# A two-layer hybrid decoder trunk on one core: the first weights split in turn with x, a bank of its own for the last block's sum, and transposes inside the next product group

## The chip, the cores and the metric

The kernel runs as one program on one core of a Trainium2 chip. Its time is the device time of one execution, in microseconds (us). The core has five engines that run their own instruction lists and wait for each other through semaphores: TensorE (PE in the profile, with the weight loads apart as PEld), VectorE (DVE), ScalarE (ACT), GpSimd (POOL) and SyncE (SP). A queue that starts DMA transfers has the engine's name with a q behind it (SPq, ACTq).

## The reference

x has 256 rows of 2048 columns, all in fp32. Two layers follow each other, and each does:

```
h  = rmsnorm(x);  z = h @ w_in          # GLU pair | q, k, v | forget logits | gates A, B
yA = conv(GLU) -> layernorm -> silu -> @ w_conv_out
yB = softmax(q k^T / sqrt(d) + C[t] - C[s], causal) v -> @ w_attn_out
x += (sigmoid(gA) * yA + sigmoid(gB) * yB) @ w_out
x += swiglu(rmsnorm(x))                 # w_gate_up, w_down, 5632 hidden columns
x += sigmoid(rmsnorm(x) @ w_ple_gate) * (p[i] @ w_ple_proj)
```

A last rmsnorm ends it. The weights are some 570 MB, which is what the profile shows as read from HBM.

## The kernel before, in words

**Split products.** A product of fp32 precision is made of three matmuls of a rounded type: x is held as xh + xl, a weight piece as wh + wl, and `Sum.add` issues xh·wh, xh·wl and xl·wh (lines 184, 185, 186), each 128x128 by 128x512. A weight piece (128 x 1024 elements, 512 KB) is brought by `fetch` into one of 8 `raw` buffers and split: ScalarE writes wh (line 143), VectorE writes wl = raw - wh (line 144). There are 5 buffers for wh and 5 for wl. A piece that is used whole feeds 12 matmuls.

**PSUM.** Two tiles of two banks ("mm") hold sums of both 128-row blocks of x. Four single banks ("ms") hold everything small: transposes, attention scores, and the product sums below. All eight banks are so in use.

**Product phases.** `fast_chunks` computes two neighbouring column chunks together by a scheme of Strassen's kind: for each group it adds and subtracts quarter pieces of the weights (lines 269 and 270 on `raw` tiles, and one DMA that adds) and issues seven products of six matmuls each: p1, c21, c11, q7, q6, q5, c12. p1, q7, q6 and q5 have a single bank each, which takes all four; c11, c12 and c21, c22 share the two mm tiles. Ordinary pieces (`go`, 12 matmuls each) are put between the products. After the products, p1 is copied from its bank by ScalarE (line 289) and VectorE combines it with the q sums. Some phases have one group, some two (`FAST = (2, 1)`).

**Transposes.** A result that is to be the next stage's left operand is transposed by TensorE: 8 transposes of 128x128 (line 330) into two single banks (`turned`), which ScalarE copies as hi (line 317, or 320 with a gain, or 349 and 352 into the operands of a product group, `Fast.take`) and VectorE subtracts as lo (lines 318, 321). Such a step is put into the list `turns`, and `run()` takes one step from it. In the kernel before, `go` calls `run()` only once the products of the phase are issued (`state["quiet"]`).

**Order.** A scheduling layer reorders the instructions of each engine when the program is built, and gives out the buffers in that order; what it made is fixed in the program. Instructions of one engine run in that order.

**Opening and end.** `fetch_first` brings the first two weight pieces, the first in two halves through the ACT queue; `take` makes xh, xl from the transposed x that `load_x` brings, scaled by the norm vector `vecs`; `warm` issues matmuls on ones. The last `fast_chunks` of the program (with `by_block`) ends one 128-row block before the other, so that the last normalisation of block 0 (lines 975 to 979) runs beside block 1's matmuls. c21 and c22 are there the two banks of one tile.

Of the kernel before, what the change touches and what calls it, by code (L numbers as in the profile page):

```python
# [28 lines left out]
KD = D // P  # L29
# [3 lines left out]
FFN_PARTS = (3, 4, 4)  # L33

PAIRS = 28
WARM = 10
RAWS = 8

FAST = (2, 1)
# [8 lines left out]
def trunk(ctx, tc, xT, xR, pT, wI, wF, wC, wA, wOut, wGU, wD, wPG, wPP, vec, bF, gF, out):  # L48
# [98 lines left out]

    recent = [None]

    def fetch_first(src, hook):  # L150

        parts = []
        for half in range(2):
            raw = raws.tile([P, 2, 512], F32, tag="raw", name=f"raw{next(uid)}")
            h = whs.tile([P, 2, 512], F32R, tag="wh", name=f"wh{next(uid)}")
            l = wls.tile([P, 2, 512], F32R, tag="wl", name=f"wl{next(uid)}")
            c = half * 1024
            if half == 0:
                for k in range(2):
                    nc.scalar.dma_start(raw[:, k, :], src[:, k * 512 : (k + 1) * 512])  # L160
                warm()
                hook()
            else:
                nc.sync.dma_start(raw.rearrange("p k n -> p (k n)"), src[:, c : c + 1024])
            for k in range(2):
                act.activation(h[:, k, :], raw[:, k, :], AF.Copy)  # L166
                dve.tensor_tensor(l[:, k, :], raw[:, k, :], h[:, k, :].bitcast(F32), op=ALU.subtract)
            parts.append((h, l))
        return parts

# [28 lines left out]
    def sums_of_blocks(n1, n2=None):  # L199
        t = once(bank_mm)  # L200
        return t, Sum(n1, lambda: t()[:, 0, :]), Sum(n1 if n2 is None else n2, lambda: t()[:, 1, :])
# [11 lines left out]
            run()  # L213


    def chunk(groups, xs, hook=None):
        n = sum(len(ks) for _, ks in groups)
        if n == 2:
            sums = [Sum(n, once(bank_ms)) for _ in range(2)]
        else:  # L220
            t, *sums = sums_of_blocks(n)
        for src, ks in groups:
            if hook is not None:
                parts = fetch_first(src, hook)
                hook = None
            else:
                parts = [split(fetch(src[:, o * 512 : (o + 2) * 512])) for o in range(0, len(ks), 2)]
            await_x(xs, ks)
            for j, p in enumerate(parts):
                plain(sums, xs, ks[2 * j], p)  # L230
            run()
            fill(CONV)
        return t() if n > 2 else [b.t for b in sums]
# [4 lines left out]
    def fast_chunks(fast, w1, w2, xs, ks, first, by_block=None):  # L238
# [4 lines left out]
        p1, q5, q6, q7 = (Sum(nf, once(bank_ms)) for _ in range(4))  # L243
        c1, c11, c12 = sums_of_blocks(nf + nk)
        c2, c21, c22 = sums_of_blocks(nf + nk, nk)
        left = deque()
        for w, sums in ((w1, (c11, c12)), (w2, (c21, c22))):
            for g, k0 in enumerate(ks):
# [23 lines left out]
        for g, f in enumerate(fast):  # L272
            a11, sm = fetch(w1[g][:, :1024]), fetch(w2[g][:, :1024])
            nc.gpsimd.dma_start(sm.rearrange("p k n -> p (k n)"), w1[g][:, :1024], accum_op=ALU.add)
            a22, a12 = fetch(w2[g][:, 1024:]), fetch(w1[g][:, 1024:])
            product(p1, f(B11), a11)
            product(c21, f(N4X), a22)
            go()
            product(c11, f(B21), a12)
            if len(left) > 2 * len(ks):  # L280
                go()
            product(q7, f(T3), sm)
            add(sm, sm, a22)
            product(q6, f(T2), sm)
            sub(a11, sm, a11)
            product(q5, f(M1), a11)
            add(a12, a12, sm)
            product(c12, f(B22), a12)
# [22 lines left out]
        return [(w[g], range(4 * g, 4 * g + 4)) for g in range(n)]  # L311


    def halves(o, src, scale=None):
        hi, lo = o[..., :S], o[..., S:]
        if scale is None:
            act.activation(hi, src, AF.Copy)
            dve.tensor_tensor(lo, src, hi.bitcast(F32), op=ALU.subtract)
        else:
            act.activation(hi, src, AF.Copy, scale=scale)  # L320
            dve.scalar_tensor_tensor(lo, src, scale, hi.bitcast(F32), op0=ALU.mult, op1=ALU.subtract)

    def turned(src):

# [155 lines left out]
            xT[:, 4 * q + lo : 4 * q + hi, :].rearrange("p k s -> p (k s)"),  # L480
        )

    def take(q, lo=0, hi=4):
        for k in range(lo, hi):
            if k % 2 == 0:
                o = pair(F32R)
                norm.tiles[4 * q + k], norm.tiles[4 * q + k + 1] = o[:, 0, :], o[:, 1, :]
            norm.xs[4 * q + k] = by_blocks(norm.tiles[4 * q + k])
            halves(
                norm.tiles[4 * q + k], xin[q].rearrange("p a b -> p (a b)")[:, k * S : (k + 1) * S],  # L490
                norm.gain(4 * q + k),
            )

    load_x(0, 0, 2)
    nc.sync.dma_start(vecs[:, :KD], vec[:, :KD])

    def warm():

# [1 line left out]
        t = bank_ms()  # L500
        for _ in range(WARM):
            pe.matmul(t[:, :P], lhsT=ones, rhs=ones, start=True, stop=True)

    def hook():
        load_x(0, 2, 4)
        take(0)

    def early():
        norm.fast = [Fast()]
# [27 lines left out]
    for i in range(L):  # L537
# [4 lines left out]
        col = lambda n: vecs[:, n : n + 1]  # L542


        def project(c, hook=None):
            return chunk(by_four(wI[i, c]), norm.xs, hook)


        u, cv = [], []
# [33 lines left out]
        for hh in range(2):  # L583
            first = i == 0 and hh == 0
            if first:
                turns.append(lambda: (load_x(1), turns.append(rest(1))))
            pa = project(GLU[hh], hook if first else None)
            at, gt = pair(), pair()
            act.activation(at, pa, AF.Copy)
            pg = project(GLU[hh] + 1)  # L590
# [463 lines left out]
```

## Time and profile before

| | |
|---|---|
| time, median of 3 runs | 2826.44 us (2826.43 to 2826.75) |
| profiled execution | 2827.59 us, of it 2825.9 us span |
| mean granted TensorE clock | 0.997 |
| TensorE busy | 2803.7 us, 99% of the span |
| VectorE busy | 2345.7 us, 83% |
| ScalarE busy | 1581.5 us, 56% |

The span is what the profile covers; 1.69 us of the profiled execution lie outside it. Busy shares tell which engine is nearly always at work; where the others are waited for is told by the waits and the timeline.

### The profile page before, as it was taken

What the parts mean: (1) busy time and instruction counts of PE and PEld (TensorE: products, weight loads), DVE (VectorE), ACT (ScalarE), POOL (GpSimd) and SP (SyncE); (2) the same over time, 40 slices, a digit from 0 to 9 for tenths busy, and PEclk for the clock granted to TensorE, in tenths of its full rate; (3) what the DMA queues carried; (4) which work ended last, traced back from release to release, by engine and by line L of the source; (5) the groups of instructions that cost most, each with busy time, mean ns of one, the idle gap of its engine ahead of it and who ended that gap; (6) DMA issues with size and microseconds to landing.
All of it is one profiled execution on the core that took longest, in us unless ns stands there. A gap on an engine that the chain in (4) does not pass through costs nothing.

```text
span 2825.9 us, 34767 instructions
## 1 busy us (share of the span) xinstructions
PE 2803.7 (99%) x12684; PEld 2318.0 (82%) x12684; DVE 2345.7 (83%) x2835; ACT 1581.5 (56%) x1912; POOL 60.0 (2%) x99
## 2 busy tenths in 40 slices
PE   9999999999999999999999999999999999999998
PEld 7888788888888888888888887888888888888886
DVE  6998877777989878888869988678689889788887
ACT  6445755565556545556644457455555465455665
POOL 0000000000000000000000000000000000000000
PEclk9999999999999999999999999999999999999999
DMA  8555466566676666666655545665656676576673
GB/s 296 183 183 187 152 215 199 192 208 192 216 224 221 203 216 217 215 216 201 214 173 189 185 165 179 209 200 180 227 188 210 220 228 221 192 231 210 204 238 123
DMA packets 158428, 573.71 MB, mean 203 GB/s; under 512 B 17840, under 2 KB 18096, under 8 KB 158000
## 3 DMA queue, kind: packets, MB, share of 16 engines
q1 hardware_dynamic: 149040, 539.50, 55.7%
q0 software_dynamic: 8352, 30.41, 5.9%
q8 instruction: 99, 1.62, 0.2%
q10 hardware_dynamic: 864, 1.57, 0.2%
q14 instruction: 73, 0.60, 0.1%
HBM read 569.32 MB, written 2.10 MB: 202 GB/s over the span
## 4 chain that ended last, share of the span: by engine, by line
PE 91%; DVE 6%; ACT 1%; issue 1%; DMA 0%; SPq 0%; POOLq 0%; POOL 0%; DVEq 0%; ACTq 0%
PE mm L184 26%; PE mm L186 26%; PE mm L185 26%; PE ms L184 4%; PE ms L185 4%; PE ms L186 4%; DVE pair L561 3%; DVE wl L144 2%; PE ms L330 2%; ACT wh L143 1%; PE ms L718 0%; DVE raw L269 0%; PE ms L747 0%; PE ms L737 0%; DMA pair<-in_xT_dram 0%
## 5 line engine op out<-in xcount | busy, mean ns | idle before, releaser
L143 ACT ACTIVATE wh<-raw 128x1024 fp32r<-128x1024 f32 x1188 | 1239.9, 1059 | 1122.4 <-PE mm L186 750.7
L144 DVE TENSOR_TENSOR wl<-raw,wh 128x1024 fp32r<-128x1024 f32 x1188 | 1434.9, 1224 | 380.8 <-ACT wh L143 375.4
L184 PE MATMUL mm<-wh,pair 128*128 128x512 f32 x3452 | 1352.9, 392 | 6.1 <-ACT wh L166 3.0
L186 PE MATMUL mm<-wh,pair 128*128 128x512 f32 x3452 | 1346.0, 390 | 0.0
L185 PE MATMUL mm<-wl,pair 128*128 128x512 f32 x3452 | 1345.7, 390 | 0.3 <-DVE wl L144 0.3
L184 PEld LDWEIGHTS mm<-wh,pair 128*128 128x128 f32 x3452 | 648.8, 188 | 139.7 <-ACT wh L166 3.2
L186 PEld LDWEIGHTS mm<-wh,pair 128*128 128x128 f32 x3452 | 648.7, 188 | 135.3
L185 PEld LDWEIGHTS mm<-wl,pair 128*128 128x128 f32 x3452 | 648.9, 188 | 133.3 <-DVE wl L144 0.7
L561 DVE SCALAR_TENSOR_TENSOR pair<-pair,vecs,pair 128x256 f32<-128x256 f32 x480 | 203.6, 492 | 0.0
L184 PE MATMUL ms<-wh,pair 128*128 128x512 f32 x496 | 193.5, 391 | 1.9 <-ACT wh L143 1.9
L186 PE MATMUL ms<-wh,pair 128*128 128x512 f32 x496 | 193.1, 389 | 0.0
L185 PE MATMUL ms<-wl,pair 128*128 128x512 f32 x496 | 193.1, 389 | 0.0
L269 DVE TENSOR_TENSOR raw<-raw,raw 128x1024 f32<-128x1024 f32 x116 | 141.8, 1222 | 1.9
L184 PEld LDWEIGHTS ms<-wh,pair 128*128 128x128 f32 x496 | 93.1, 188 | 23.6 <-ACT wh L143 3.0
L186 PEld LDWEIGHTS ms<-wh,pair 128*128 128x128 f32 x496 | 93.0, 188 | 19.4
L185 PEld LDWEIGHTS ms<-wl,pair 128*128 128x128 f32 x496 | 93.1, 188 | 18.8
L269 DVE TENSOR_TENSOR pair<-pair,ms 128x512 f32<-128x512 f32 x144 | 94.2, 683 | 0.0
L270 DVE TENSOR_TENSOR pair<-mm,pair 128x1024 f32<-128x1024 f32 (+1 forms) x49 | 59.0, 1203 | 18.9 <-PE mm L186 18.9
L270 DVE TENSOR_TENSOR raw<-raw,raw 128x1024 f32<-128x1024 f32 x58 | 71.0, 1225 | 1.9
L269 DVE TENSOR_TENSOR pair<-pair,mm 128x1024 f32<-128x1024 f32 x48 | 58.5, 1219 | 11.9 <-PE mm L186 11.9
L330 PEld LDWEIGHTS ms<-ident,pair 128*128 128x128 f32 x336 | 39.1, 140 | 5.6
L330 PE MATMUL ms<-ident,pair 128*128 128x128 f32 x336 | 43.5, 272 | 0.0
(166 smaller groups left out, 1027.8 us busy)
## 6 DMA issues: line engine op xcount, KB each, us to landing
raw<-in_wGU_dram SPq DMA_DIRECT2D x352, 512.0 KB, 4.8
raw<-in_wI_dram SPq DMA_DIRECT2D x287, 512.0 KB, 3.9
raw<-in_wD_dram SPq DMA_DIRECT2D x176, 512.0 KB, 5.4
raw<-in_wOut_dram SPq DMA_DIRECT2D x64, 512.0 KB, 4.7
raw<-in_wPG_dram SPq DMA_DIRECT2D x64, 512.0 KB, 4.9
raw<-in_wA_dram SPq DMA_DIRECT2D x32, 512.0 KB, 4.3
raw<-in_wC_dram SPq DMA_DIRECT2D x32, 512.0 KB, 5.1
raw<-in_wGU_dram POOLq DMA_DIRECT2D x30, 512.0 KB, 8.2
```

Of the source, the lines that this page charges most:

```text
L143: act.activation(h, raw, AF.Copy)
L144: dve.tensor_tensor(l, raw, h.bitcast(F32), op=ALU.subtract)
L184: pe.matmul(self.t, lhsT=xh, rhs=wh, start=start, stop=False)
L185: pe.matmul(self.t, lhsT=xh, rhs=wl, start=False, stop=False)
L186: pe.matmul(self.t, lhsT=xl, rhs=wh, start=False, stop=self.left == 0)
L269: add = lambda o, a, b: dve.tensor_tensor(o, a, b, op=ALU.add)
L270: sub = lambda o, a, b: dve.tensor_tensor(o, a, b, op=ALU.subtract)
L330: pe.transpose(pt[:, kk * S + b * P : kk * S + (b + 1) * P], src(b)[:, c : c + P], ident)
L561: dve.scalar_tensor_tensor(cv[c], u[c][:, j : j + S], w, cv[c], op0=ALU.mult, op1=ALU.add,)
```

## The change

Four edits. In `fetch_first`, the halves of the first two pieces and the halves of x are split in turn, in an order that is kept (`keep_in_program_order`), and all of the first x tile is asked for before; `WARM` is 14 in place of 10. The norm vectors are loaded ahead of x. In the last `fast_chunks`, c22 has a single bank. In every `fast_chunks`, one `run()` is issued in the first group, after the second `go` and ahead of q7.

```diff
--- before.py
+++ after.py
@@ -33,7 +33,7 @@
 FFN_PARTS = (3, 4, 4)
 
 PAIRS = 28
-WARM = 10
+WARM = 14
 RAWS = 8
 
 FAST = (2, 1)
@@ -147,9 +147,10 @@
 
     recent = [None]
 
-    def fetch_first(src, hook):
+    def fetch_first(src):
 
         parts = []
+        keep = tc.keep_in_program_order
         for half in range(2):
             raw = raws.tile([P, 2, 512], F32, tag="raw", name=f"raw{next(uid)}")
             h = whs.tile([P, 2, 512], F32R, tag="wh", name=f"wh{next(uid)}")
@@ -159,12 +160,13 @@
                 for k in range(2):
                     nc.scalar.dma_start(raw[:, k, :], src[:, k * 512 : (k + 1) * 512])
                 warm()
-                hook()
+                load_x(0, 2, 4)
             else:
                 nc.sync.dma_start(raw.rearrange("p k n -> p (k n)"), src[:, c : c + 1024])
             for k in range(2):
-                act.activation(h[:, k, :], raw[:, k, :], AF.Copy)
-                dve.tensor_tensor(l[:, k, :], raw[:, k, :], h[:, k, :].bitcast(F32), op=ALU.subtract)
+                keep(act.activation(h[:, k, :], raw[:, k, :], AF.Copy))
+                keep(dve.tensor_tensor(l[:, k, :], raw[:, k, :], h[:, k, :].bitcast(F32), op=ALU.subtract))
+                take(0, 2 * half + k, 2 * half + k + 1, keep)
             parts.append((h, l))
         return parts
 
@@ -213,16 +215,16 @@
             run()
 
 
-    def chunk(groups, xs, hook=None):
+    def chunk(groups, xs, first=False):
         n = sum(len(ks) for _, ks in groups)
         if n == 2:
             sums = [Sum(n, once(bank_ms)) for _ in range(2)]
         else:
             t, *sums = sums_of_blocks(n)
         for src, ks in groups:
-            if hook is not None:
-                parts = fetch_first(src, hook)
-                hook = None
+            if first:
+                parts = fetch_first(src)
+                first = False
             else:
                 parts = [split(fetch(src[:, o * 512 : (o + 2) * 512])) for o in range(0, len(ks), 2)]
             await_x(xs, ks)
@@ -243,6 +245,8 @@
         p1, q5, q6, q7 = (Sum(nf, once(bank_ms)) for _ in range(4))
         c1, c11, c12 = sums_of_blocks(nf + nk)
         c2, c21, c22 = sums_of_blocks(nf + nk, nk)
+        if by_block is not None:
+            c22 = Sum(nk, once(bank_ms))
         left = deque()
         for w, sums in ((w1, (c11, c12)), (w2, (c21, c22))):
             for g, k0 in enumerate(ks):
@@ -279,6 +283,8 @@
             product(c11, f(B21), a12)
             if len(left) > 2 * len(ks):
                 go()
+            if g == 0:
+                run()
             product(q7, f(T3), sm)
             add(sm, sm, a22)
             product(q6, f(T2), sm)
@@ -311,14 +317,14 @@
         return [(w[g], range(4 * g, 4 * g + 4)) for g in range(n)]
 
 
-    def halves(o, src, scale=None):
+    def halves(o, src, scale=None, done=lambda op: op):
         hi, lo = o[..., :S], o[..., S:]
         if scale is None:
             act.activation(hi, src, AF.Copy)
             dve.tensor_tensor(lo, src, hi.bitcast(F32), op=ALU.subtract)
         else:
-            act.activation(hi, src, AF.Copy, scale=scale)
-            dve.scalar_tensor_tensor(lo, src, scale, hi.bitcast(F32), op0=ALU.mult, op1=ALU.subtract)
+            done(act.activation(hi, src, AF.Copy, scale=scale))
+            done(dve.scalar_tensor_tensor(lo, src, scale, hi.bitcast(F32), op0=ALU.mult, op1=ALU.subtract))
 
     def turned(src):
 
@@ -480,7 +486,7 @@
             xT[:, 4 * q + lo : 4 * q + hi, :].rearrange("p k s -> p (k s)"),
         )
 
-    def take(q, lo=0, hi=4):
+    def take(q, lo=0, hi=4, done=lambda op: op):
         for k in range(lo, hi):
             if k % 2 == 0:
                 o = pair(F32R)
@@ -488,11 +494,11 @@
             norm.xs[4 * q + k] = by_blocks(norm.tiles[4 * q + k])
             halves(
                 norm.tiles[4 * q + k], xin[q].rearrange("p a b -> p (a b)")[:, k * S : (k + 1) * S],
-                norm.gain(4 * q + k),
+                norm.gain(4 * q + k), done,
             )
 
+    nc.sync.dma_start(vecs[:, :KD], vec[:, :KD])
     load_x(0, 0, 2)
-    nc.sync.dma_start(vecs[:, :KD], vec[:, :KD])
 
     def warm():
 
@@ -500,10 +506,6 @@
         t = bank_ms()
         for _ in range(WARM):
             pe.matmul(t[:, :P], lhsT=ones, rhs=ones, start=True, stop=True)
-
-    def hook():
-        load_x(0, 2, 4)
-        take(0)
 
     def early():
         norm.fast = [Fast()]
@@ -542,8 +544,8 @@
         col = lambda n: vecs[:, n : n + 1]
 
 
-        def project(c, hook=None):
-            return chunk(by_four(wI[i, c]), norm.xs, hook)
+        def project(c, first=False):
+            return chunk(by_four(wI[i, c]), norm.xs, first)
 
 
         u, cv = [], []
@@ -584,7 +586,7 @@
             first = i == 0 and hh == 0
             if first:
                 turns.append(lambda: (load_x(1), turns.append(rest(1))))
-            pa = project(GLU[hh], hook if first else None)
+            pa = project(GLU[hh], first)
             at, gt = pair(), pair()
             act.activation(at, pa, AF.Copy)
             pg = project(GLU[hh] + 1)
```

**TensorE, first product phase of the down projection in layer 1 (the page's time 748 us).** Before, the last three matmuls of q7 (tile ms1176), then those of q6 (ms1179):

```order
L186 MATMUL ms1176_6262<-wh1174_6258,pair1053_5664 128x512
L184 MATMUL ms1179_6274<-wh1177_6270,pair1052_5663 128x512
L185 MATMUL ms1179_6274<-wl1178_6271,pair1052_5663 128x512
L186 MATMUL ms1179_6274<-wh1177_6270,pair1053_5664 128x512
L184 MATMUL ms1179_6274<-wh1177_6270,pair1052_5663 128x512
L185 MATMUL ms1179_6274<-wl1178_6271,pair1052_5663 128x512
L186 MATMUL ms1179_6274<-wh1177_6270,pair1053_5664 128x512
L184 MATMUL ms1182_6286<-wh1180_6282,pair1052_5663 128x512
L185 MATMUL ms1182_6286<-wl1181_6283,pair1052_5663 128x512
```

Now, from the transposes on (ms1174 and ms1176 are the transposed tiles, ms1180 is q7, ms1183 is q6, mm1168 with wh1187 and wl1188 is c12; line numbers are two higher for the sums and six higher for the transposes):

```order
L336 MATMUL ms1174_6262<-ident_85,pair1081_5839 128x128 x4
L336 MATMUL ms1176_6270<-ident_85,pair1081_5839 128x128 x4
L186 MATMUL ms1180_6282<-wh1178_6278,pair1038_5598 128x512
L187 MATMUL ms1180_6282<-wl1179_6279,pair1038_5598 128x512
L188 MATMUL ms1180_6282<-wh1178_6278,pair1039_5599 128x512
L186 MATMUL ms1180_6282<-wh1178_6278,pair1038_5598 128x512
L187 MATMUL ms1180_6282<-wl1179_6279,pair1038_5598 128x512
L188 MATMUL ms1180_6282<-wh1178_6278,pair1039_5599 128x512
L186 MATMUL mm1168_6221<-wh1187_6314,pair1036_5594 128x512
L187 MATMUL mm1168_6221<-wl1188_6315,pair1036_5594 128x512
L186 MATMUL ms1183_6294<-wh1181_6290,pair1038_5598 128x512
L187 MATMUL ms1183_6294<-wl1182_6291,pair1038_5598 128x512
```

The eight transposes stand ahead of q7, and two matmuls of c12 stand between q7 and q6. In the program, q6's first matmul now waits for the copy of p1 (line 295), whose bank it is given, and q5's for the subtraction of the first transposed tile (line 324).

**ScalarE at the same place.** Before, wh of q7, the copy of p1 (line 289), wh of q6, q5, c12 and of the next ordinary pieces:

```order
L143 ACTIVATE wh1174_6258<-raw1156_6182 128x1024
L289 ACTIVATE pair1153_6178<-ms1161_6193 128x512
L143 ACTIVATE wh1177_6270<-raw1156_6182 128x1024
L143 ACTIVATE wh1180_6282<-raw1155_6180 128x1024
L143 ACTIVATE wh1183_6294<-raw1158_6187 128x1024
L143 ACTIVATE wh1186_6311<-raw1185_6309 128x1024
L143 ACTIVATE wh1193_6345<-raw1192_6343 128x1024
```

Now, wh of q7, q6, q5, c12, then the copies of the two transposed tiles (line 323), then the copy of p1 (line 295) and the next wh:

```order
L143 ACTIVATE wh1178_6278<-raw1156_6186 128x1024
L143 ACTIVATE wh1181_6290<-raw1156_6186 128x1024
L143 ACTIVATE wh1184_6302<-raw1155_6184 128x1024
L143 ACTIVATE wh1187_6314<-raw1158_6191 128x1024
L323 ACTIVATE pair1175_6267<-ms1174_6262 128x2x256
L323 ACTIVATE pair1177_6275<-ms1176_6270 128x2x256
L295 ACTIVATE pair1153_6182<-ms1161_6197 128x512
L143 ACTIVATE wh1190_6331<-raw1189_6329 128x1024
```

The copy of p1 moved from behind q7's wh to behind c12's wh and two more copies.

**ScalarE in the opening.** Before, the four pieces of x (line 320, pair10 and pair11), then the four of the weights (line 166):

```order
L320 ACTIVATE pair10_135<-pair1_110,vecs_83 128x256 x2
L320 ACTIVATE pair11_140<-pair1_110,vecs_83 128x256 x2
L166 ACTIVATE wh6_117<-raw5_116 128x512 x2
L166 ACTIVATE wh13_150<-raw12_149 128x512 x2
L143 ACTIVATE wh17_185<-raw16_183 128x1024
```

Now in turn, one of the weights (line 167) and one of x (line 326):

```order
L167 ACTIVATE wh6_117<-raw5_116 128x512
L326 ACTIVATE pair10_141<-pair1_110,vecs_83 128x256
L167 ACTIVATE wh6_117<-raw5_116 128x512
L326 ACTIVATE pair10_141<-pair1_110,vecs_83 128x256
L167 ACTIVATE wh12_149<-raw11_148 128x512
L326 ACTIVATE pair14_154<-pair1_110,vecs_83 128x256
L167 ACTIVATE wh12_149<-raw11_148 128x512
L326 ACTIVATE pair14_154<-pair1_110,vecs_83 128x256
L143 ACTIVATE wh17_189<-raw16_187 128x1024
```

The first piece of the weights moved from behind four pieces of x to the front. On SP's queue the norm vectors are first, and the next x tile is asked for behind one more weight piece than before.

## Rows read from the trace of the kernel before

**Rows 1.** The page: busy time of each engine, share of the span, instructions.

```profile
PE 2803.7 (99%) x12684; PEld 2318.0 (82%) x12684; DVE 2345.7 (83%) x2835; ACT 1581.5 (56%) x1912; POOL 60.0 (2%) x99
```

**Rows 2.** What TensorE waited for, over the span (us in total, times, longest).

```profile
PE mm L184 <- ACT wh L166: 3.0, 1, 3.0
PE ms L184 <- ACT wh L143: 1.9, 2, 1.0
PE mm L184 <- ACT wh L143: 1.3, 2, 0.7
...
PE mm L184 <- ACT pair L317: 1.1, 2, 0.5
```

**Rows 3.** TensorE in two stretches of the opening: busy time, granted clock, DMA.

```profile
7.60:14.30 6.70, 6.26 (x14) 0.50 1.01 384
...
14.40:20.00 5.60, 5.60 (x26) 1.00 1.03 420
```

**Rows 4.** Timeline of TensorE in the opening: start, us, engine, line, tiles, idle before.

```profile
8.04 0.79 PE L184 MATMUL mm<-wh,pair 128*128 128x512 f32 x1 [2.96 <-ACT wh L166]
...
17.19 0.39 PE L186 MATMUL mm<-wh,pair 128*128 128x512 f32 x1
```

**Rows 5.** Timeline of ScalarE in the opening.

```profile
5.41 0.91 ACT L320 ACTIVATE pair<-pair,vecs 128x256 fp32r<-128x256 f32 x2 [2.18 <-DMA vecs<-in_vec_dram]
...
7.38 2.17 ACT L166 ACTIVATE wh<-raw 128x512 fp32r<-128x512 f32 x4
...
11.50 1.71 ACT L320 ACTIVATE pair<-pair,vecs 128x256 fp32r<-128x256 f32 x4
```

**Rows 6.** Timeline of TensorE, end of the first product phase of the down projection.

```profile
748.47 0.39 PE L184 MATMUL ms<-wh,pair 128*128 128x512 f32 x1
...
753.92 1.04 PE L330 MATMUL ms<-ident,pair 128*128 128x128 f32 x8
754.71 0.47 PE L184 MATMUL mm<-wh,pair 128*128 128x512 f32 x1
755.72 0.50 PE L184 MATMUL mm<-wh,pair 128*128 128x512 f32 x1 [0.53 <-ACT pair L317]
756.05 0.39 PE L185 MATMUL mm<-wl,pair 128*128 128x512 f32 x1
```

**Rows 7.** Timeline of VectorE in the same phase.

```profile
739.15 1.22 DVE L270 TENSOR_TENSOR pair<-mm,pair 128x1024 f32<-128x1024 f32 x1 [0.35 <-PE mm L186]
...
747.59 1.22 DVE L269 TENSOR_TENSOR raw<-raw,raw 128x1024 f32<-128x1024 f32 x1
...
750.02 1.23 DVE L144 TENSOR_TENSOR wl<-raw,wh 128x1024 fp32r<-128x1024 f32 x1
```

**Rows 8.** Timeline of ScalarE in the same phase.

```profile
748.92 4.89 ACT L143 ACTIVATE wh<-raw 128x1024 fp32r<-128x1024 f32 x5 [1.25 <-DVE raw L269]
...
755.08 1.07 ACT L317 ACTIVATE pair<-ms 128x512 fp32r<-128x512 f32 x2
```

**Rows 9.** Timeline of another product phase: TensorE at q7, then VectorE.

```profile
531.20 0.39 PE L184 MATMUL ms<-wh,pair 128*128 128x512 f32 x1
...
531.25 3.65 DVE L144 TENSOR_TENSOR wl<-raw,wh 128x1024 fp32r<-128x1024 f32 x3
```

**Rows 10.** Timeline of the gate phase in the attention stretch: ScalarE, then TensorE.

```profile
297.84 1.28 ACT L840 ACT_TABLE_LOAD   x1
299.13 0.73 ACT L840 ACTIVATE pair<-pair,rt 128x512 f32<-128x512 f32 x1
...
310.49 0.50 PE L184 MATMUL ms<-wh,pair 128*128 128x512 f32 x1 [0.96 <-ACT wh L143]
```

**Rows 11.** Timeline of the end: TensorE, then VectorE.

```profile
2808.57 0.50 PE L184 MATMUL mm<-wh,pair 128*128 128x512 f32 x1 [0.78 <-DVE pair L270]
...
2813.03 0.89 DVE L975 TENSOR_SCALAR xt<-xt,rt 128x512 f32<-128x512 f32 x2 [0.70 <-POOL rt L442]
2814.36 0.69 DVE L270 TENSOR_TENSOR pair<-mm,pair 128x512 f32<-128x512 f32 x1 [0.44 <-PE mm L186]
```

## Prediction

> **What bounds the kernel now.** I read the page first: TensorE is busy for 99% of the span, VectorE for 83%, ScalarE for 56% [rows 1]. So a microsecond is won only where TensorE stands still or runs slowly, and lost wherever the change makes it stand still. The list of its waits comes second: the largest is 3.0 us at the start, then 1.9 + 1.3 us for weight halves of ScalarE and 1.1 us for transposed tiles [rows 2]. Third, the granted clock by stretch: TensorE runs at half (1.2 of 2.4 GHz) from 7.6 to 14.3 us, at full speed after it [rows 3]. Last I read the timelines of the places that the edits touch [rows 4 to 11]. Away from these places matmuls follow each other every 0.227 us: 24 of them from 748.47 to 753.92 [rows 6].
>
> **The opening.** TensorE's first real matmul is at 8.04 [rows 4], because wh comes on ScalarE only after four pieces of x, at 7.38, and the x pieces wait for `vecs` until 5.41 [rows 5]. In turn, ScalarE needs 0.54 us for a weight half (2.17 for four) and 0.46 for a piece of x (0.91 for two) [rows 5]. From 5.41 at the latest, the first pair is ready at about 6.4; the transfer of `vecs` is now first in its queue, so I take 6.2. The first 24 matmuls are then bound by the splits, some 1.05 us per k, and end near 12. The 25th needs the next x tile, scaled from 11.50 on today [rows 5], but asked for one 512 KB piece later now: at 420 GB/s [rows 3] 1.25 us, so it lands near 12.75, its hi is there at 13.3 and the lo, behind one more split on VectorE, at 14.2. The 27th matmul, today at 17.19 [rows 4], comes at about 14.2: **3.0 us less**. Four more warm matmuls on ones lie under the wait for the first weights, and cost nothing unless they outlast 6.2 us. If the clock falls again while TensorE waits for the second tile, and for as long as today (6.7 us with 14 matmuls of twice the length [rows 3]), some 3 us are lost again: the bounds are 0 and 3.0 us less. I take 3.0, since that wait (1.3 us) is nearer to the 0.96 us of [rows 10], behind which a matmul takes 0.50 us and not 0.79 as at 8.04, than to today's 2.96 us [rows 4].
>
> **The end.** With its own bank, block 1's sum no longer waits 0.78 us for block 0's subtraction [rows 11]. But block 1's subtraction today waits only 0.44 us for TensorE, behind line 975 on VectorE [rows 11]; what is earlier than that stands behind line 975. So **0.4 us less**, 0 to 0.8.
>
> **Transposes earlier: what is gained.** In the down projection the last operand's tiles are transposed at 753.92 and wanted at once: from 754.71 the next matmul comes after 1.01 us in place of 0.23 [rows 6], 0.78 us in each of two layers, **1.6 us less**. In the attention stretch the second gate phase loses about 2.6 us per layer, of which the waits at wh are 1.0 and 0.7 [rows 2, 10]. ScalarE has three table loads for sigmoid and softmax ahead of q7's wh there; in the new order one is left, and the softmax is done ahead of it. VectorE, with layernorm pieces between, still brings c12's wl late: I estimate 1.3 us left, and 0.6 us new in the phase before it (next part). That is 0.75 us won per layer, **1.5 us less**, with bounds of 4 less and 2 more for both.
>
> At this point the Trainium skill has another price ("ScalarE: Activation LUTs", What ACT_TABLE_LOAD costs): some 1.28 us for the load and 1.38 us for a drain, 2.66 us per switch. The trace agrees with the load, 1.28 us, but the next activation starts at 299.13, 0.01 us after it [rows 10], so no drain shows here. By the page, the load that is left would cost 1.4 us more per layer and nothing would be won in this stretch: 1.5 us more in the sum. The trace decides.
>
> **Transposes earlier: what it costs.** This is the largest term. With both transposed tiles taken before q7, p1, the two tiles and q7 fill the four single banks, and q6 must be given one of them. The order rows of the change say which: q6 waits for p1's copy, which ScalarE now does behind c12's wh and two copies, and q5 for VectorE's subtraction of the first tile, behind c12's wl; two matmuls of c12 are pulled ahead of q6 and need c12's wl too. Today that wl has cover: c12 is the fourth product, 4.08 us after q7's start.
>
> Step by step in the phase at 748 us. Transposes take 0.79 us (753.92 to 754.71 [rows 6]), so q7 starts at 748.47 + 0.79 and ends at 750.62. c12's first matmul goes, its second should start at 750.85. It needs c12's wl, which VectorE computes from 750.02 to 751.25 [rows 7]; this chain starts at 739.15 from a sum that TensorE ended long before the transposes [rows 7], and does not move. So TensorE stands 0.45 us. The first matmul after a wait gives the next one only after 0.33 us, not 0.23 (755.72 to 756.05 [rows 6]): 0.10 us more. On ScalarE, c12's wh starts at 748.92 [rows 8], waiting for VectorE's sum of 747.59 [rows 7], and takes 0.98 (five in 4.89); two copies take 1.07 and p1's about 0.58, so p1's bank is free at 751.5 [rows 8], just as the two c12 matmuls are through. The loss is **0.55 us**.
>
> I went through the new TensorE order for all such phases. In each layer 15 phases outside attention have transposes before q7. In two, the bank comes from copies of ScalarE alone and comes in time. In eight, it is the pattern above, with p1's copy or the tile's subtraction as the last; in three with two groups four matmuls of c12 come first, with the same wl. In the last two, which build a product operand, about 3.6 us of VectorE work are put ahead of the second group's splits, which costs about as much. In the phase at 531 us VectorE stands to q7 much as it does here (q5's wl starts 0.05 us after q7 [rows 9]), and p1's copy, counted in the same way, gives 0.55 us there too. So 13 phases per layer, 26 in all, at 0.55: **14.3 us more**. The bounds are 0.25 us a phase (6.5 us), if ScalarE or VectorE run ahead of today, and 0.7 us (18 us), if both waits add up.
>
> The sum: -3.0 - 0.4 - 1.6 - 1.5 + 14.3 = **7.8 us more**. The profiled execution took 2827.59 us with its span of 2825.9, 1.15 us more than the median of the runs; against it this gives 2835.4, against the median of 2826.44 it gives **2834.2 us**.
>
> **Rivals.**
> - *The bank waits are half hidden.* If VectorE's chain starts earlier against TensorE than today, because the tile's subtractions no longer stand behind the products, c12's wl comes some 0.3 us earlier and a phase loses 0.25 us: 6.5 - 6.5 = 0, about 2826.5, no change. Against it: in the phase at 748 us that chain starts with a wait for TensorE's own sum [rows 7].
> - *Faster.* The gains are 6.5 us. If q6's bank is free and c12's wl is there before TensorE gets to them, nothing of the 14.3 is paid: 2819.9. The point that decides is 0.03 us per phase: beyond it the gain falls under 5.65 us, which is 0.2% and about what a measurement of this kernel can tell from no change. For it speaks that ScalarE is idle 44% of the time [rows 1]; against it, that its instructions stand in a fixed order and c12's wh waits for VectorE [rows 8].
> - *Slower still.* The clock falls again in the opening, and the attention stretch wins nothing: 4.5 us more, 2838.7. For it speaks that TensorE waits in the opening in any case; against it, that the wait is half as long.
>
> **How the numbers follow.** The forecast, waits of about 0.55 us in 26 places, has 0.58; its own range is 2830 to 2838, for 0.45 to 0.65 us a phase and the bounds of the opening. Half hidden has 0.19, faster 0.11, slower still 0.12. 0.2% is 2820.8 to 2832.1. The forecast lies above that in 0.47 of its 0.58; so slower is 0.47 + 0.12 = 0.59, same 0.11 + 0.19 = 0.30, faster 0.11. The range 2826 to 2840 leaves out the faster case and the edges, under 2 in 10.
>
> **What would show it.** In the changed profile's waits, new rows at the sums' bank tiles: "ms" matmuls of line 186 waiting for line 295 or 324, and "mm" of line 187 waiting for wl of line 144, some 10 us together. The timeline near 748 us: eight transposes, six matmuls, one, a gap of about 0.45 us. The row at 755.72 without its wait. The opening: first real matmul near 6.2, granted clock 1.00 through it, a wait of about 1.3 us near 12. The end: line 975 directly before block 1's subtraction. I am wrong if TensorE's matmuls after the transposes follow without a gap, or if p1's copy is done before q7 ends.

## The result and the profile after

| | before | after |
|---|---|---|
| time, median (range, runs) | 2826.44 us (2826.27 to 2827.47, 5) | 2838.64 us (2836.89 to 2841.56, 5) |
| profiled execution | 2827.59 us, span 2825.9 | 2836.89 us, span 2835.2 |
| mean granted TensorE clock | 0.997 | 0.999 |

The ratio is 1.0042, with an interval of 1.0031 to 1.0052: the change makes the kernel slower by 0.42%, 12.2 us. The profiled execution of after is the fastest of its five, 1.75 us under their median, and that of before is 1.15 us over its own, so in the profiles only 9.3 us of the 12.2 are to be found.

The page of after, first part, answers to [rows 1]. Every engine's share is as before; shares don't tell where the time went.

```profile
PE 2810.5 (99%) x12692; PEld 2314.8 (82%) x12692; DVE 2348.9 (83%) x2835; ACT 1576.3 (56%) x1912; POOL 60.1 (2%) x99
```

TensorE's waits in after (us in total, times, longest), against [rows 2]:

```profile
PE mm L187 <- DVE wl L144: 6.9, 21, 1.1
...
PE ms L186 <- ACT pair L295: 0.7, 4, 0.2
PE mm L188 <- DVE pair L327: 0.5, 1, 0.5
...
PE ms L186 <- DVE pair L324: 0.4, 2, 0.2
...
PE mm L186 <- ACT wh L143: 0.2, 1, 0.2
```

The 3.0 us at the start and the 3.2 us for ScalarE's weight halves are gone but for 0.2. In their place stand 21 waits for wl of line 144, of which one, the longest, is in the opening at 41 us, and the two kinds of wait for a bank: on line 295 (p1's copy) and on line 324 (the tile's subtraction).

**Opening.** TensorE in five stretches of the opening: busy time, granted clock, DMA share, GB/s. The clock is 1.00 all through, where [rows 3] had 0.50.

```profile
6.00:8.00 2.00, 1.98 (x10) 1.00 0.86 329
8.00:10.00 2.00, 1.61 (x8) 1.00 1.02 414
10.00:12.00 2.00, 2.00 (x9) 1.00 1.04 424
12.00:14.00 2.00, 1.65 (x7) 1.00 1.03 422
14.00:16.00 2.00, 1.69 (x7) 1.00 1.03 420
```

TensorE's timeline there, and again at 41 us. The row at 6.17 is the first real matmul, the one at 9.63 the 13th, the one at 14.31 the 27th, which [rows 4] had at 17.19; the rows at 41 us have no counterpart among the rows of before.

```profile
6.17 0.50 PE L186 MATMUL mm<-wh,pair 128*128 128x512 f32 x1
...
9.63 0.50 PE L186 MATMUL mm<-wh,pair 128*128 128x512 f32 x1 [0.39 <-ACT pair L326]
...
14.31 0.50 PE L188 MATMUL mm<-wh,pair 128*128 128x512 f32 x1 [0.53 <-DVE pair L327]
...
41.41 0.50 PE L186 MATMUL mm<-wh,pair 128*128 128x512 f32 x1
43.01 0.50 PE L187 MATMUL mm<-wl,pair 128*128 128x512 f32 x1 [1.11 <-DVE wl L144]
```

**A product phase.** TensorE in the phase of [rows 6], 1.82 us earlier now since the opening and the attention of layer 1 have won more than was lost up to here:

```profile
746.65 1.03 PE L336 MATMUL ms<-ident,pair 128*128 128x128 f32 x8
747.44 0.47 PE L186 MATMUL ms<-wh,pair 128*128 128x512 f32 x1
...
748.67 0.39 PE L188 MATMUL ms<-wh,pair 128*128 128x512 f32 x1
748.90 0.40 PE L186 MATMUL mm<-wh,pair 128*128 128x512 f32 x1
749.46 0.50 PE L187 MATMUL mm<-wl,pair 128*128 128x512 f32 x1 [0.16 <-DVE wl L144]
749.80 0.40 PE L186 MATMUL ms<-wh,pair 128*128 128x512 f32 x1
```

Read the starts, not the bracket: from 748.90 to 749.46 are 0.56 us where 0.23 is the rule, and 0.34 to the next, so 0.33 + 0.11 = 0.44 us are lost. The bracket shows only 0.16, because the modelled end of the matmul before reaches into the gap. So the 6.9 us of the list of waits are less than what the waits cost.

ScalarE there, against [rows 8], then VectorE, against [rows 7]:

```profile
747.09 1.06 ACT L143 ACTIVATE wh<-raw 128x1024 fp32r<-128x1024 f32 x1 [1.25 <-DVE raw L273]
748.06 1.07 ACT L323 ACTIVATE pair<-ms 128x512 fp32r<-128x512 f32 x2
749.01 0.60 ACT L295 ACTIVATE pair<-ms 128x512 f32<-128x512 f32 x1
```

```profile
746.89 2.52 DVE L144 TENSOR_TENSOR wl<-raw,wh 128x1024 fp32r<-128x1024 f32 x2
749.33 1.29 DVE L324 TENSOR_TENSOR pair<-ms,pair 128x512 fp32r<-128x512 f32 x2
```

c12's wl, the second of the two, is ready at 749.41 and its matmul starts at 749.46. p1's copy ends at 749.61; q6's first matmul, which takes its bank, starts at 749.80. Without its wait, c12's second matmul could have started at about 749.13 and q6 at 749.36, and q6 would have waited for that copy instead: two waits lie over each other.

**Where the time went, phase by phase.** TensorE computes the same products in each phase of both profiles, so the start of p1 in after minus that in before adds up what was won and lost so far. The last column is an experiment told of below.

| p1 starts, before | after | after - before | p1_one - before |
|---|---|---|---|
| 246.27 | 244.67 | -1.60 | -1.21 |
| 391.16, behind attention, layer 1 | 387.97 | -3.19 | -3.21 |
| 738.95 | 737.12 | -1.83 | -2.79 |
| 1649.02, ahead of attention, layer 2 | 1653.26 | +4.24 | -3.40 |
| 1793.96, behind it | 1796.63 | +2.67 | -5.46 |
| 2672.69, last phase | 2681.59 | +8.90 | -5.73 |
| end of the span, 2825.9 | 2835.2 | +9.3 | -5.6 |

So the opening wins 1.6 in these two profiles and attention 1.6 in each layer. The opening's size differs between executions: the 27th matmul is 2.25 to 3.40 us earlier than in this profile of before in the eight profiles of kernels with the new opening (those told of below with after), and in the two others with the old one it is 0.89 earlier (`c22_only`) and 0.06 later (`turn_only`). Between 391 and 1649 us 7.4 are lost net, and from 1794 to the last phase 6.2.

### The profile page after: what moved, and what is told of

Its sections match the earlier page's. It is cut to its first block, busy times and chain, and to the rows that moved or that the text cites. A ratio compares the mean times of both kernels' runs of the same rounds, so it can differ in the third digit from the quotient of the medians.

```text
span 2835.2 us, 34833 instructions
## 1 busy us (share of the span) xinstructions
PE 2810.5 (99%) x12692; PEld 2314.8 (82%) x12692; DVE 2348.9 (83%) x2835; ACT 1576.3 (56%) x1912; POOL 60.1 (2%) x99
## 4 chain that ended last, share of the span: by engine, by line
PE 81%; DVE 13%; issue 3%; ACT 2%; DMA 1%; POOL 0%; SPq 0%; ACTq 0%; POOLq 0%; DVEq 0%
PE mm L187 23%; PE mm L188 23%; PE mm L186 23%; DVE wl L144 5%; PE ms L186 3%; PE ms L187 3%; PE ms L188 3%; DVE pair L563 2%; DVE raw L273 2%; ACT wh L143 2%; DVE raw L274 1%; PE ms L336 1%; DVE pair L914 1%; PE ms L720 0%; DVE pair L374 0%
## 5 line engine op out<-in xcount | busy, mean ns | idle before, releaser
L186 PE MATMUL ms<-wh,pair 128*128 128x512 f32 x508 | 201.7, 398 | 1.1 <-ACT pair L295 0.7
L188 PE MATMUL ms<-wh,pair 128*128 128x512 f32 x508 | 198.1, 390 | 0.0
```

The source lines that it names most:

```text
L186: pe.matmul(self.t, lhsT=xh, rhs=wh, start=start, stop=False)
L188: pe.matmul(self.t, lhsT=xl, rhs=wh, start=False, stop=self.left == 0)
```

## Experiments

Each kernel is timed in five rounds beside the kernel before.

**Is it the moved step, and does the rest win?** `no_turn` is after without the moved step; `turn_only` is before with that step alone.

```diff
# no_turn, against after
-            if g == 0:
-                run()
# turn_only, against before
+            if g == 0:
+                run()
             product(q7, f(T3), sm)
```

> The changed kernel without the run() in the first group; the opening, the norm vectors' place and c22's own bank stay. Theory (the bank wait): all of the loss is in the product phases that have transposes ahead of q7, so what is left is the opening's 2.9 us less 1.0 us that is given back near 41 us, and 0.4 us at the end: 2826.4 - 2.3 = 2824.1 us. Rival (the loss is in the opening, whose rows only look better, through weights that come later): no better than 2826.4 us, with the late weights still there. TensorE's waits: no row of line 187 for wl with more than two or three entries.

> The kernel before with the run() in the first group alone. Theory (the bank wait): the changed kernel's 2838.6 us and back what the opening and the end won, 2.3 us: 2840.9 us, with the same 20 or so waits of the second matmul of a weight piece for wl, 0.45 us of TensorE each. Rival (two edits together make the loss, such as the opening moving all that follows against the DMA queue): close to 2826.4 us, within 3 us.

`no_turn`: 2825.60 us (2825.22 to 2826.15), ratio 0.9995, interval 0.9987 to 1.0004, before 2826.80. `turn_only`: 2840.05 us (2838.44 to 2842.05), ratio 1.0047, 1.0034 to 1.0059. The parts add up: -1.2 + 13.2 = 12.0 of 12.2 us. The whole slowdown is the moved step's. The first wait of `turn_only` is

```profile
PE mm L185 <- DVE wl L144: 6.7, 21, 0.8
```

as often as in after, and in `no_turn` one such wait is left, that at 41 us:

```profile
PE mm L187 <- DVE wl L144: 1.1, 1, 1.1
```

`no_turn` came out 1.5 us above its expectation. The wait at 41 us was counted there already, with 1.0 us. Of the 1.5, the kernel before was itself 0.4 us slower in these rounds; for the rest the profile shows that the opening won less in this execution: 2.43 us at the 27th matmul and 1.1 at 246 us, where after has 2.88 and 1.6.

**Is it p1's bank?** After has p1 copied behind the products. `p1_early` has ScalarE copy it just ahead of the transposes, and does the moved step in the last group; in a phase of one group that is the place it has in after, so there only the copy differs.

```diff
# p1_early, against after
-            if g == 0:
+            if g == len(fast) - 1:
+                act.activation(u1[:, 0, :], p1.t, AF.Copy)
                 run()
             product(q7, f(T3), sm)
...
-        act.activation(u1[:, 0, :], p1.t, AF.Copy)
```

> The changed kernel with run() in the last group of a phase in place of the first, and p1's copy issued right before it, so that p1's bank is free again when q6 needs one; the transposes and all of their copies and subtractions stay ahead of q7 or near it. Theory (the bank wait): q6 follows q7 at once, c12 is no longer pulled ahead of it, and the 15.8 us that the product phases lost between the two traces are back: 2838.6 - 15.8 = 2822.8 us, faster than the kernel before. Rival (work of ScalarE and VectorE that is moved ahead of the splits makes them late, whatever the banks): the same work stands at the same place, so 2835 us or more.

2824.69 us (2824.26 to 2825.43), ratio 0.9992, 0.9983 to 1.0001: some 14 us below after, and 1.9 above the expectation. TensorE in the phase of above, then ScalarE:

```profile
747.07 0.48 PE L186 MATMUL ms<-wh,pair 128*128 128x512 f32 x1
...
748.30 0.39 PE L188 MATMUL ms<-wh,pair 128*128 128x512 f32 x1
748.53 0.39 PE L186 MATMUL ms<-wh,pair 128*128 128x512 f32 x1
```

```profile
738.32 0.60 ACT L287 ACTIVATE pair<-ms 128x512 f32<-128x512 f32 x1 [0.30 <-PE ms L188]
```

p1 is copied as soon as its sum ends, q6's bank is free, and q6 follows q7 after 0.23 us. c12 is the fourth product again, so nobody waits for its wl, though VectorE's chain stands to TensorE as in after (two tiles' subtractions 0.66 us after q7's last start, in both). So the waits for wl that lead the list are a consequence (all but the one at 41 us, which stays): with no bank for q6, the order has c12 ahead of it, before its wl. The ten phases of two groups lose 0.33 us each here, which the expectation had left out.

**Which phases?** `p1_one` does the moved step in phases of one group alone; those of two groups are as before. `p1_split` keeps the early copy in the former, and treats the latter as after does.

```diff
# p1_one, against after
-            if g == 0:
+            if len(fast) == 1:
+                act.activation(u1[:, 0, :], p1.t, AF.Copy)
                 run()
...
-        act.activation(u1[:, 0, :], p1.t, AF.Copy)
+        if len(fast) > 1:
+            act.activation(u1[:, 0, :], p1.t, AF.Copy)
# p1_split, against p1_one
+            if len(fast) == 1:
+                act.activation(u1[:, 0, :], p1.t, AF.Copy)
+            if g == 0:
                 run()
```

> As the run with p1's copy early, but run() is issued, and p1 copied, only in phases of one group; phases of two groups have their transposes after the products, as in the kernel before. Theory (the bank wait, by what each phase lost against the kernel before in the trace of that run: 0.33 us in each of ten phases of two groups): 2824.7 - 3.3 = 2821.4 us. Rival (transposes inside a group win nothing but the down projection's 0.8 us and the attention stretch): the same, so this run measures a size; a time of 2824 us or more would say that the ten phases lose elsewhere.

> As the run before it in this list, but phases of two groups have run() in their first group as in the changed kernel, where p1 is not complete and its bank can't be had; q6 must wait for a transposed tile there. Theory (the bank wait): what those phases lost in the changed kernel comes back, 0.45 us in three and 1.05 us in two per layer, 3.4 us per layer: 2821.4 + 6.9 = 2828.3 us, with waits of line 187 for wl in ten places. Rival (p1's late copy is all of it): 2822 us.

`p1_one`: 2821.43 us (2821.11 to 2822.00), ratio 0.9981, 0.9972 to 0.9990, as expected; its column in the table above wins at the opening, twice at attention and 0.8 us in each down projection, and between them loses only some 0.5 us per layer, most of it (0.36) in the phase at 566 us. `p1_split`: 2831.15 us (2830.17 to 2833.20), ratio 1.0016, 1.0007 to 1.0025: 9.7 us more, from the two-group phases and what follows them, and 2.9 more than expected. So of the 17.2 us between after and `p1_one`, some 7.5 (2838.64 - 2831.15) are p1's late copy in phases of one group, and 9.7 the moved step in phases of two. By the trace, three phases of two groups per layer lose 0.44 us each; the two that build a product operand (p1 starts at 845 and 1099 us in layer 1) lose 0.82, not the 1.05 of the expectation; and the phase behind each of these two, which the expectation had left out, loses 0.4 to 1.15 us. TensorE in one of the latter, at the last matmul of q6 and the first of q5, then VectorE:

```profile
1153.16 0.39 PE L188 MATMUL ms<-wh,pair 128*128 128x512 f32 x1
1154.19 0.50 PE L186 MATMUL ms<-wh,pair 128*128 128x512 f32 x1 [0.64 <-DVE pair L327]
```

```profile
1151.01 2.52 DVE L144 TENSOR_TENSOR wl<-raw,wh 128x1024 fp32r<-128x1024 f32 x2
1153.45 1.28 DVE L327 TENSOR_TENSOR pair<-ms,pair 128x512 fp32r<-128x512 f32 x2
```

Here the bank that is late is q5's, freed by line 327, and VectorE's splits start 0.47 us after q7 (1150.54); in the usual phase of after they start 0.55 us before it (746.89 to 747.44). In after itself that phase is the dearest: q7 starts at 1152.55, the same two splits at 1153.02, and c12 loses 1.34 us:

```profile
1154.33 0.50 PE L186 MATMUL mm<-wh,pair 128*128 128x512 f32 x1 [0.15 <-ACT wh L143]
1155.59 0.51 PE L187 MATMUL mm<-wl,pair 128*128 128x512 f32 x1 [0.76 <-DVE wl L144]
```

Here, behind a phase that builds a product operand, VectorE stands 1.0 us later to TensorE than in the usual phase (0.47 + 0.55), and this phase pays for it. The usual phase at 747 us lies behind a phase of two groups too, but one that builds none.

**Does after wait differently from run to run?** `after_again` is the same kernel.

> The changed kernel once more, for a second profile of it. Theory (its larger spread from run to run comes from the waits for wl in the phases that follow two-group phases, where VectorE is behind): the phases near 897, 1154, 2306 and 2563 us lose other amounts than in the first profile, the rest the same to 0.1 us. Rival (the spread is in transfers or the clock): differences all over the span, or another granted clock.

2838.68 us (2838.01 to 2840.11), ratio 1.0042, 1.0028 to 1.0056. Its profiled span is 2838.1 us, 2.9 longer than that of the first profile. Phase by phase, it is 0.5 us ahead of it from the opening on, and then it loses 1.15 us more between the p1 starts at 887 and 930 (times of before), 0.18 between 1141 and 1184, 0.26 between 2290 and 2333, and 1.45 between 2544 and 2587; anywhere else the difference between the two moves by less than 0.1 us. The first of these places in the first profile of after, then in `after_again`:

```profile
898.32 0.52 PE L187 MATMUL mm<-wl,pair 128*128 128x512 f32 x1 [0.38 <-DVE wl L144]
```

```profile
897.78 0.50 PE L186 MATMUL mm<-wh,pair 128*128 128x512 f32 x1 [0.17 <-ACT wh L143]
899.04 0.50 PE L187 MATMUL mm<-wl,pair 128*128 128x512 f32 x1 [0.76 <-DVE wl L144]
```

So the executions differ in the four phases behind those that build a product operand; in that ahead of 2587, c12's first matmul stands 0.79 us ahead of its second in the first profile, 1.26 in the other, which also has one wait of 0.36 us more, on VectorE. The kernels with these waits (after, `turn_only`, `p1_split`) spread over 2.1 to 4.7 us, those without over 0.5 to 1.4, the kernel before over 1.2 to 1.7.

VectorE is later there because ScalarE is: in `after_again` it waits 1.60 us for wh at 884.64 and 1.87 us at 2552.23, and in the first profile not at all in these two stretches. ScalarE in turn waits for a weight piece. The wh ahead of the first and of the last of the four phases, in after, then in `after_again`:

```profile
882.20 1.06 ACT L143 ACTIVATE wh<-raw 128x1024 fp32r<-128x1024 f32 x1 [1.85 <-DMA raw<-in_wGU_dram]
...
2546.88 1.06 ACT L143 ACTIVATE wh<-raw 128x1024 fp32r<-128x1024 f32 x1 [1.05 <-DMA raw<-in_wGU_dram]
```

```profile
883.54 4.35 ACT L143 ACTIVATE wh<-raw 128x1024 fp32r<-128x1024 f32 x4 [3.67 <-DMA raw<-in_wGU_dram]
...
2551.14 4.11 ACT L143 ACTIVATE wh<-raw 128x1024 fp32r<-128x1024 f32 x4 [3.94 <-DMA raw<-in_wGU_dram]
```

| phase whose p1 starts in before at | ScalarE's wait, after; after_again | the phase loses, after; after_again |
|---|---|---|
| 887 | 1.85; 3.67 | 0.71; 1.86 |
| 1141 | 3.40; 3.56 | 1.58; 1.75 |
| 2290 | 2.94; 3.16 | 1.11; 1.36 |
| 2544 | 1.05; 3.94 | 0.66; 2.11 |

In all eight, the longer the wait, the larger the loss, and the wh starts within 0.15 us of the piece's landing. (The profile puts the 3.16 down to TensorE, but there too the piece lands just before.) In `p1_one`, ScalarE waits for a transfer at none of the four places, in the kernel before only at the third, for 0.50 us. So the theory had the places right, and the rival the source: transfers, though not all over the span. Why a piece lands sooner in one execution than in another stays open, and no run tests it.

**Are the four more warm matmuls needed?** `warm10` is `no_turn` with `WARM = 10`.

> The changed kernel without run() in the first group, and with WARM at 10 again. TensorE then waits from about 5.1 to 6.2 us for the first weights and x. If the four more warm matmuls are not needed: granted clock 1.00 all through the opening and the time of the run without run(), 2825.6 us. If they are: the clock falls as in the kernel before, and some 3 us are lost, 2828.6 us.

2825.32 us (2825.25 to 2825.70), ratio 0.9995, 0.9986 to 1.0003, as `no_turn`. Its granted clock between the warm matmuls and 8 us:

```profile
5.10:8.00 2.90, 2.69 (x12) 1.00 0.99 342
```

They are not needed. What is left as the reason is the earlier first pair, at 6.05 us in place of 8.04, behind a wait of 0.21 us: in the three profiles with the old opening waits of 2.96 (before), 2.59 (`c22_only`) and 2.44 us (`turn_only`) came ahead of the first pair, and then matmuls 0.43 us apart. That is a comparison of profiles; no run changes the wait alone.

**What gives back the opening's gain?** ScalarE, then VectorE, in after, ahead of the wait at 43.01. The seven squares for the norm (line 422) stand from 36.01 to 39.69 without anything between.

```profile
36.01 0.61 ACT L422 ACTIVATE tmp<-xt 128x512 f32<-128x512 f32 x1
...
39.69 0.62 ACT L422 ACTIVATE tmp<-xt 128x512 f32<-128x512 f32 x1
...
40.31 1.99 ACT L143 ACTIVATE wh<-raw 128x1024 fp32r<-128x1024 f32 x2
```

```profile
41.62 0.47 DVE L690 TENSOR_SCALAR rq<-rt 128x2 f32<-128x2 f32 x1 [0.83 <-POOL rt L448]
41.73 2.36 DVE L144 TENSOR_TENSOR wl<-raw,wh 128x1024 fp32r<-128x1024 f32 x2
```

In the order of after, seven squares come ahead of two weight halves on ScalarE, and on VectorE an instruction that waits 0.83 us for the norm's end stands ahead of their wl. The first of the two wh ends at 41.35 (40.31 and 1.04), and its wl starts at 41.73, so some 0.4 of the 1.37 us below are this instruction's, and the rest ScalarE's. In before, weight halves stand between the squares, and TensorE loses 0.45 us at 38.50 (0.68 to the next matmul) in place of 1.37 (1.60 from 41.41). `squares_apart` is `p1_one` with the squares issued in two steps:

```diff
-        for n in range(N4):
+        for n in range(2):
+            norm.squares(n)
+        turns.append(more)
+
+    def more():
+        for n in range(2, N4):
             norm.squares(n)
         norm.finish()
```

> As the run with run() only in phases of one group, and the squares of x in the opening are issued in two steps in place of one, so that fewer of them stand ahead of the weight halves on ScalarE near 40 us. Theory (the 1.1 us wait for wl near 41 us comes from seven squares in a row ahead of two wh): that wait shrinks to under 0.3 us, 2821.4 - 1.3 = 2820.1 us. Rival (it comes from wl standing behind the small VectorE operation that waits for GpSimd there): the wait stays at 1 us, 2821.4 us.

2820.06 us (2819.52 to 2820.40), ratio 0.9976, 0.9967 to 0.9985: 1.37 us below `p1_one`, faster than both kernels. ScalarE has a weight half after the fifth square:

```profile
39.32 1.04 ACT L143 ACTIVATE wh<-raw 128x1024 fp32r<-128x1024 f32 x1
...
40.88 1.04 ACT L143 ACTIVATE wh<-raw 128x1024 fp32r<-128x1024 f32 x1
```

and no wait for wl is left in TensorE's list. The edit moves the norm's end behind the squares too (VectorE's instruction is at 44.29 now), so the run does not separate the theory from its rival; only the rows above do, by their 0.4 us.

**The end alone.** `c22_only` is before with a bank of its own for c22.

```diff
+        if by_block is not None:
+            c22 = Sum(nk, once(bank_ms))
```

> The kernel before with c22's own bank alone. Theory: block 1's subtraction came 0.44 us after line 975 of block 0 for want of TensorE's sum; with its own bank the sum is there 0.8 us earlier and line 975 is the last: 2826.7 - 0.4 = 2826.3 us, with the 0.78 us wait at the end gone. Rival (the tail behind it, from the last normalisation on, is what ends last, whatever TensorE does): no change.

2826.29 us (2825.98 to 2827.35), ratio 0.9999, 0.9990 to 1.0007, before 2826.88. TensorE's wait of 0.78 us is gone, and block 1's subtraction stands directly behind line 977 on VectorE, as [rows 11] let expect:

```profile
2812.12 0.88 DVE L977 TENSOR_SCALAR xt<-xt,rt 128x512 f32<-128x512 f32 x2 [0.69 <-POOL rt L444]
2812.92 0.69 DVE L272 TENSOR_TENSOR pair<-ms,pair 128x512 f32<-128x512 f32 x1
```

By the rows the end wins 0.3 us and not 0.4: from block 0's line 977 (975 in before) to block 1's it is 6.21 us in place of 6.50, since block 1's subtraction starts 0.53 earlier, and VectorE then waits 1.03 us for ScalarE in place of 0.79. The times can't tell so little from nothing.

## Why the prediction was right

The direction and the mechanism were right. The time lies in the outer range, 2826 to 2840 us, and 0.6 us above the forecast's own, 2830 to 2838; the sum gave 7.8 us more and the runs 12.2. That it is no further off is in part luck: the opening was put 1.4 us too high and attention 1.7 too low, and a usual phase too dear while eight others were too cheap. By its steps:

- **The opening, -3.0.** At the 27th matmul it is 17.19 - 14.31 = 2.88 us, with the first matmul at 6.17 (6.2 forecast) and the clock at 1.00. So near is luck too, since the executions spread from 2.25 to 3.40. The wait of 1.3 us near 12 did not come; there are two, of 0.39 and 0.53 us. And the term ended at 14 us. At 41 us 1.15 are lost again (1.37 in place of 0.45 at the wait, and 0.23 just ahead of it), and with the 0.11 of starting again at 14.31 that leaves -1.6 at 246 us. `squares_apart` shows that the place of the squares and of the norm's end behind them is the cause.
- **The end, -0.4.** The wait is gone and block 1's subtraction stands where it was forecast; by the rows 0.3 us are won, since some of it is lost again behind it. No time can confirm the size.
- **The down projection's stall, -1.6.** The row that stood at 755.72 [rows 6] has no counterpart in after's list of waits, so 0.78 us per layer, as forecast (0.80 and 0.76 in `p1_one`).
- **Attention, -1.5.** Under-sized: 1.6 us per layer, -3.2 in all. In layer 1, -1.60 at 246.27 becomes -0.63 at the p1 of 297.63 and -3.19 at 391.16: the first gate phase costs 1.0 and not 0.6, and the second wins all of its 2.6, where 1.3 us of waiting for wl were forecast to stay. ScalarE there, where one table load is left ahead of q7's wh (the row at 300.56), as was forecast; before, three stand ahead of it, at 297.84, 299.88 and 302.18:

```profile
298.02 1.28 ACT L842 ACT_TABLE_LOAD   x1
299.32 1.34 ACT L842 ACTIVATE pair<-pair,rt 128x512 f32<-128x512 f32 x2
300.56 1.04 ACT L143 ACTIVATE wh<-raw 128x1024 fp32r<-128x1024 f32 x1
```

  The load takes 1.28 us and the next activation starts 0.02 us after it. The Trainium skill ("ScalarE: Activation LUTs", What ACT_TABLE_LOAD costs) adds a drain of 1.38 us to a switch; neither of the two profiles shows one at this load, and the stretch did not lose what it would cost.
- **The bank waits, +14.3.** This is the term that was mis-sized; its mechanism held, and `p1_early` shows it, since with p1's bank free in time neither q6 nor c12 waits. In the usual phase the loss is 0.44 us, not 0.55 (the gap is 0.33, not 0.45; by the prediction's own starts, 751.25 - 750.85, it would be 0.40). What was taken as the same in all 26 phases is not: the four that build a product operand pay 0.82 each, and the four behind them 0.66 to 1.58 in the first profile and 1.36 to 2.11 in the second, where ScalarE waits for a weight piece and VectorE for ScalarE. These eight cost 7.3 and 10.4 us, where 8 x 0.55 = 4.4 were forecast. From the profile, all is 9.3 + 1.6 + 0.3 + 1.6 + 3.2 = 16.0 us, 0.62 a phase; from the runs of `turn_only`, 13.2 + 1.6 + 3.2 = 18.0, or 0.69. That is the upper bound that was given, 0.7, though not for its reason: in most phases the two waits lie over each other, and do not add up.

The rivals: *half hidden* and *faster* asked for c12's wl or q6's bank earlier against TensorE; VectorE's splits kept their place in the usual phase (c12's wl is ready 1.97 us after q7's start, 1.99 by the prediction's rows), and in some phases fell behind. *Slower still* came to nearly the measured time by other means: the clock did not fall and attention won. Its two parts are both refuted, and what is 4 us above the forecast is the phases that build a product operand and those behind them, for which the prediction traced the order of the instructions and not how late ScalarE and VectorE stand.

## What to carry to other kernels

When work is pulled forward between two products, ask first whose bank it takes and who frees it: a copy of 0.6 us, issued where its result was wanted, cost some 7.5 us in the phases of one group, more than the four gains together by the profile (6.7), and issued where its sum ended it cost nothing there. The wait that leads the list (wl) need not be the cause, since an order may have been turned round a missing bank. After an earlier start, follow the shift from phase to phase until it is constant; here 1.15 of 2.88 us were lost again 27 us later. And where one profile shows a wait that another execution has longer, follow it back over the engines: here it led from TensorE over VectorE and ScalarE to a weight piece that landed late.

## What the runs showed of the hardware

- With in-turn splits TensorE has short waits in the opening (0.39 us ahead of the 13th matmul, 0.53 ahead of the 27th) and the granted clock stays at 1.00; in before, a wait of 2.96 us was followed by 0.50 until 14.3 us [rows 3, 4]. `c22_only`, with the opening of before, has matmuls 0.43 us apart until 12.16 only, where before has them until 14.05, and is 0.89 us ahead of it from 16 us on. In `turn_only` they are 0.43 us apart until 13.87 though its granted clock reads 1.00 there: the spacing of the matmuls has to be read with the clock.
- Two executions of one program can differ by the landing of a few weight pieces: the two profiles of after keep their difference to less than 0.1 us over most phases, and change it by 3.0 us in four of them, in which ScalarE waits 1.05 to 3.40 us for a piece in the first and 3.16 to 3.94 in the second.
